# Macaron FFN, attention and RG-LRU block on one core: where the output projection's weight splits stand, and which attention unit a recurrent piece follows

## The chip, the cores and the metric

The kernel runs on one core of a Trainium2 chip. The metric is device time in microseconds (us), and lower is better. Before the change the median of three runs is 2323.7 us (2322.83 to 2324.29). Five engines with separate instruction streams share the work: TensorE (PE in the profile; its weight loads are PEld), VectorE (DVE), ScalarE (ACT), GpSimd (POOL) and SyncE (SP), whose queue issues most of the DMAs here.

## The reference, cut to what matters

The input is 1024 tokens of 1024 float32 features. One layer is computed:

```
x = LN1(ALPHA*x + 0.5 * FFN1(x))
z = x @ w_in
fox = forgetting_attention(q, k, v, fg)          # 8 heads of 64, causal, with a decay per token
lru = gelu(z_lg) * rg_lru(conv(z_lx))            # recurrent half, 512 channels
x = LN2(ALPHA*x + concat([fox, lru]) @ w_out)    # the output projection
x = LN3(ALPHA*x + 0.5 * FFN2(x))
```

The output projection is a sum of two parts: rows 0 to 511 of `w_out` multiply the attention's result, rows 512 to 1023 the recurrent result.

## The kernel before

**Three products for one.** Every large product is made of three TensorE matmuls in a 32-bit format with shorter mantissa (`mm3`, lines 156 to 158). An operand is first split into a high and a low part: ScalarE casts the high part (line 148 or 283), VectorE subtracts it from the source to get the low part (line 149 or 284). The matmuls are high x high, high x low and low x high.

**Stages.** FFN1's up and gate products, FFN1's down product, the input projection with the recurrent unit (`mixer_in`), the attention with the output projection (`attention`), then FFN2 in the same two stages. The change is in `attention`.

**Units.** The attention of one head is cut into 8 units of 128 query rows. Unit (h, i) is head h with query rows i*128 to i*128+127, and sees (i+1)*128 keys. Units are numbered n = 0 to 63 in the order of the loop. Heads 0 to 5 come one after the other, each from i = 7 (1024 keys) down to i = 0 (128 keys), so n = 24 to 31 is head 3, 32 to 39 head 4, 40 to 47 head 5. The units of heads 6 and 7 are mixed: n = 48 to 51 are (6,7) to (6,4), then (7,7), (7,6), (6,3), (6,2), (7,5), (7,4) and so on.

**What a unit does.** TensorE makes the scores (lines 999 and 1000) into one of two score tiles `s`. VectorE adds the decay and takes the minimum in one pass (line 1005, `low` below; the profile calls it CUSTOM_DVE_ANT_0). ScalarE takes the exponential (line 1006). In heads 0 to 3 VectorE takes a reciprocal (line 1008) and GpSimd multiplies with it (line 1009). Three units later (two from head 4 on) TensorE transposes the result (line 1020), ScalarE casts the high part out of PSUM (line 1024) and VectorE makes the low part (line 1025). After each second unit of a head come the products with v (line 1041), whose two halves ScalarE and VectorE put together (lines 1044 and 1045). From head 5 on two more transposes bring in the reciprocals (line 1050, used on line 1051). At the end of a head pair the result is split into the `mix` tiles (lines 1053 and 1054), and for heads 0 to 5 it is stored to DRAM (line 1057).

**Pieces in between.** The recurrent rows of the output projection do not depend on the attention. They are cut into 16 pieces (8 row blocks x 2 column halves), each 12 matmuls into one PSUM bank and one VectorE add into the residual row (`down_tile`, line 222). The loop issues a piece after chosen units, so that TensorE has work while the unit's chain runs on other engines. Before, the rule is `n < 2 or n % 8 in (2, 3, 4)`, which gives n = 0 to 4, 10 to 12, 18 to 20, 26 to 28, 34 and 35.

**The attention rows.** The weights of the other half, `w_out` rows 0 to 511, are split in four steps (`out_w`, which calls `split_ws`): each is one ScalarE cast and one VectorE subtraction of 128 x 1024. The generator is advanced at n = 45, 47, 49 and 51. The `mix` results of heads 0 to 5 are loaded back from DRAM at the units in `MIXES` (line 1110); these tiles and the weight tiles reuse the memory of the recurrent tiles, so they have to wait for the last recurrent piece that reads them. After head 7's unit (7,6) the first output tiles follow: 12 matmuls per tile (lines 156 to 158 again, now with `w` of the attention rows and `mix`), two tiles per row block, then the layer norm.

**What sets the order.** The Tile layer places the instructions of each engine by its own estimate of when their operands are ready; the order of the code is a preference. `issue_after` and `issue_behind` (the latter adds a dependence without a semaphore) force an order on one engine. Each engine then runs its stream in order, and waits on semaphores. So the place of a split in the loop does not say where it stands in the ScalarE and VectorE streams, and the trace of before shows the four splits well ahead of n = 45.

Of the kernel before, what the change touches and what calls it, by code (L numbers as in the profile page):

```python
# [12 lines left out]
AF = mybir.ActivationFunctionType  # L13
ALU = mybir.AluOpType
# [34 lines left out]
def f32(ap):  # L49
    return ap.bitcast(F32)  # L50


class Block:
# [91 lines left out]
    def split_ws(self, src, k):  # L145

        hi, lo = (self.wsp.tile([P, 4 * VW], F32R, tag="ws", name=self.nm("w"))[:, 0:D].rearrange("p (k c) -> p k c", k=k) for _ in range(2))
        self.nc.scalar.copy(hi, src)
        self.nc.vector.tensor_tensor(lo, src, f32(hi), ALU.subtract)
        return hi, lo  # L150

    def mm3(self, out, lhs, rhs, first, last, goes_on=False):
# [810 lines left out]
    def attention(self, w_out, mixp, ln, normed):  # L963

        nc, v = self.nc, self.nc.vector
# [5 lines left out]
        with self.pool("att_p", 3) as pp, self.pool("att_t", 1) as tp, self.pool("att_pt", 6) as ptp, self.pool("att_qk", 2, side="right") as qkp:  # L971

            def load(h):
                vt = qkp.tile([P, NT, P], F32R, tag="v", name=self.nm("v"))
                cum = qkp.tile([P, T], F32, tag="cum", name=self.nm("cum"))
                q, kh, kl = (qkp.tile([P, T], F32R, tag=t, name=self.nm(t)) for t in ("q", "kh", "kl"))
                mine = slice(64 * (h % 2), 64 * (h % 2) + 64)
                for j in range(2):
                    rows = slice(64 * j, 64 * j + 64)
                    nc.sync.dma_start(f32(q[rows]), self.q_d[h // 2, j, mine, :])  # L980
                    nc.sync.dma_start(f32(kh[rows]), self.k_d[h // 2, 0, mine, :])
                    nc.sync.dma_start(f32(kl[rows]), self.k_d[h // 2, 1, mine, :])
                row = self.cum_d[h:h + 1, :]
                nc.sync.dma_start(cum, bass.AP(tensor=row.tensor, offset=row.offset, ap=[[0, P], [1, T]]))
                self.last_load = nc.sync.dma_start(f32(vt), self.v_d[h].rearrange("(j p) d -> p j d", p=P))
                return q, kh, kl, vt, cum

            sums, inv = self.fgz, self.wf.rearrange("p h i -> p (h i)").rearrange("p (h i) -> p h i", h=HEADS)

            def probs(h, i):  # L990

                q, kh, kl, _, cum = heads[h]
                n = (i + 1) * P
                ts = slice(i * P, n)
                s = self.s_tile()
                for bank in range((n + H - 1) // H):
                    c1 = min(max(n - bank * H, 256), H)
                    cols = slice(bank * H, bank * H + c1)
                    mm(s[:, bank, 0:c1], q[:, ts], kh[:, cols], start=True, stop=False)
                    scores = mm(s[:, bank, 0:c1], q[:, ts], kl[:, cols], start=False, stop=True)  # L1000
                sf = s.rearrange("p b c -> p (b c)")
                p = pp.tile([P, T], F32, tag="p", name=self.nm("p"))
                nc.gpsimd.affine_select(cum[:, ts], cum[:, ts], pattern=[[-1, P]], compare_op=ALU.is_ge, fill=1e30, base=0, channel_multiplier=1)
                m = self.small.tile([P, 4], F32, tag="m", name=self.nm("m"))
                v.tensor_tensor_reduce(p[:, 0:n], sf[:, 0:n], cum[:, 0:n], 1.0, 3e38, ALU.add, ALU.min, m[:, 1:2])
                nc.scalar.activation(p[:, 0:n], p[:, 0:n], AF.Exp, bias=m[:, 1:2], scale=-1.0, accum_out=sums[:, h, i:i + 1])
                if h < LAST:
                    v.reciprocal(m[:, 3:4], sums[:, h, i:i + 1])
                    nc.gpsimd.tensor_scalar(p[:, 0:n], p[:, 0:n], m[:, 3:4], 1.0, op0=ALU.mult, op1=ALU.mult)
                return p, scores  # L1010

            def to_pT(h, i, p):
                if i % 2:
                    pts[h, i // 2] = [tuple(ptp.tile([P, 4, 256], F32R, tag="pt", name=self.nm("pt")) for _ in range(2))
                                      for _ in range((i + 4) // 4)]
                for g in range((i + 4) // 4):
                    js = range(4 * g, min(4 * g + 4, i + 1))
                    pa = self.a_tile()
                    for j in js:
                        nc.tensor.transpose(pa[:, (j % 4) * P:(j % 4 + 1) * P], p[:, j * P:(j + 1) * P], self.ident)  # L1020
                    w = len(js)
                    pav = pa.rearrange("p (j t) -> p j t", j=4)[:, 0:w, :]
                    hi, lo = (x[:, 0:w, (i % 2) * P:(i % 2 + 1) * P] for x in pts[h, i // 2][g])
                    nc.scalar.copy(hi, pav)
                    v.tensor_tensor(lo, pav, f32(hi), ALU.subtract)
                if h > LAST and h % 2 and i % 2 == 0:
                    r = inv[:, h - 1:h + 1, i:i + 2]
                    v.reciprocal(r, sums[:, h - 1:h + 1, i:i + 2])
                    nc.gpsimd.tensor_copy(self.gate_raw.rearrange("p u (b d) -> p u b d", b=2),
                                          r.rearrange("p b u -> p u b").unsqueeze(3).to_broadcast([P, 2, 2, 64]))  # L1030
# [28 lines left out]
            heads, pts, ps, outs, mixes = {}, {}, {}, {}, {}  # L1059
# [2 lines left out]
            units += [(6 + h, i) for h, i in ((0, 7), (0, 6), (0, 5), (0, 4), (1, 7), (1, 6), (0, 3), (0, 2),  # L1062
                                              (1, 5), (1, 4), (0, 1), (0, 0), (1, 3), (1, 2), (1, 1), (1, 0))]
            tiles, mix, w_fox, w_steps = [], [], [], self.out_w(w_out, 0)
            MIXES = 40, 50, 52
            fill = [(i, d) for i in range(NT) for d in range(2)]
            AHEAD, LAST = 3, 4

            def due(n):

                return [u for u in (n - AHEAD, n - AHEAD + 1) if 0 <= u < len(units) and u + AHEAD - (u >= LAST * NT) == n]
# [3 lines left out]
            def out_tile():  # L1075
                i, d = tiles.pop(0)
                self.down_tile(i, list(zip(mix + [mixes[3]], w_fox)), 1.0, (d,))
                if d:
                    self.layer_norm(i)
                    normed(i)  # L1080

            for n in range(len(units) + AHEAD + 1):
                if n < len(units):
                    h, i = units[n]
                    if i == 5 and h < 6 or (h, i) == (6, 6):
                        heads[h + 1] = load(h + 1)
                    if i == NT - 1:
                        if h % 2 == 0:
                            outs[h // 2] = tp.tile([P, T], F32, tag="o", name=self.nm("o"))
                        else:  # L1090
                            mixes[h // 2] = tuple(mixp.tile([P, T], F32R, tag="h", name=self.nm("mix")) for _ in range(2))
                    ps[n], scores = probs(h, i)
                for m in due(n):
                    to_pT(*units[m], ps.pop(m))
                for m in due(n - 1):
                    h, i = units[m]
                    if i % 2 == 0:
                        values(h, i // 2)
                        if h == HEADS - 1:
                            tiles += [(i + 1, 0), (i + 1, 1), (i, 0), (i, 1)]  # L1100
                if fill and (n < 2 or n % 8 in (2, 3, 4)):
                    i, d = fill.pop(0)
                    with self.tc.issue_after(scores.ins) if n < 3 else nullcontext():
                        self.down_tile(i, lru_tiles, 1.0, (d,))
                if 45 <= n < 53 and n % 2:
                    w_fox.append(next(w_steps))
                if n in MIXES:
                    mix.append(tuple(self.hp.tile([P, T], F32R, tag="h", name=self.nm("mix")) for _ in range(2)))
                    for l in range(2):
                        nc.sync.dma_start(f32(mix[-1][l]), mix_d[len(mix) - 1][l])  # L1110
                    if len(mix) == 3:
                        self.load_gb(*ln, [self.hp.tile([P, T], F32, tag="h", name=self.nm("gb")) for _ in range(2)])
                if tiles:
                    out_tile()
# [136 lines left out]
```

## Time and profile before

| quantity | value |
|---|---|
| median of 3 runs | 2323.7 us |
| the profiled execution's own time | 2323.84 us |
| its span, first to last instruction | 2322.1 us |
| TensorE busy | 2302.8 us |
| VectorE busy | 1631.8 us |
| ScalarE busy | 1012.6 us |
| granted TensorE clock | 0.999 |

The span is 1.7 us shorter than the profiled execution's own time. Busy times are read with care on TensorE: matmuls are pipelined, so a row of the timeline starts before the one ahead of it has ended (the modelled end), and a short wait can hide under a modelled end. The distance from one start to a later start is the safer measure, and it is used below for whole stretches between the score matmuls of two units. A row of the timeline gives start, duration, engine, line, operation, tiles and count; in brackets stands idle time ahead of it with what ended it.

### The profile page before, as it was taken

To read this page: it belongs to the slowest core of one execution; us is meant where nothing else is said; L and a number is where in the kernel's file an instruction comes from. 1 tells how busy PE (TensorE), PEld (TensorE's weight loads), DVE (VectorE), ACT (ScalarE), POOL (GpSimd) and SP (SyncE) were. 2 spreads that over 40 slices of the span, in tenths; PEclk is the share of its full clock that TensorE was granted. 3 is DMA by queue.
4 is the path that set the end of the run, shared out by engine and by line. 5 is a ranking of instruction groups with operands and counts; after the bars stand their busy time and mean duration, and the time that the engine had idled before them with its cause. 6 is when DMAs were issued, how large, how long until landed. Compare 5 with 4: busy or idle time off the path is not lost.

```text
span 2322.1 us, 28275 instructions
## 1 busy us (share of the span) xinstructions
PE 2302.8 (99%) x10737; PEld 1916.8 (83%) x10737; DVE 1631.8 (70%) x2489; ACT 1012.6 (44%) x1589; POOL 202.7 (9%) x344
## 2 busy tenths in 40 slices
PE   9999999999999999999999999999999999999998
PEld 7888888888888888888898787888888888888887
DVE  8766566666567788866667899665656665577886
ACT  5443333333344335454456745434333333344342
POOL 0020000000000000111133200000000000000000
PEclk9999999999999999999999999999999999999999
DMA  4333232323375433132275812232323232564542
GB/s 145 129 94 119 87 118 87 118 87 118 125 265 200 163 127 120 65 103 96 101 203 146 245 64 94 88 118 88 122 93 124 87 118 87 193 246 169 182 144 73
DMA packets 175976, 298.93 MB, mean 129 GB/s; under 512 B 8208, under 2 KB 100688, under 8 KB 175840
## 3 DMA queue, kind: packets, MB, share of 16 engines
q1 hardware_dynamic: 152768, 218.16, 28.9%
q0 software_dynamic: 23072, 78.97, 8.6%
q8 instruction: 84, 1.38, 0.2%
q14 instruction: 52, 0.43, 0.1%
HBM read 214.22 MB, written 82.87 MB: 128 GB/s over the span
## 4 chain that ended last, share of the span: by engine, by line
PE 93%; DVE 4%; ACT 1%; DMA 1%; issue 1%; SPq 0%; DVEq 0%; ACTq 0%
PE x L156 9%; PE x L158 9%; PE x L157 9%; PE b L156 7%; PE b L157 7%; PE b L158 7%; PE s L157 6%; PE s L158 6%; PE s L156 6%; PE a L158 6%; PE a L156 6%; PE a L157 6%; PE a L1041 1%; PE a L1020 1%; PE a L898 1%
## 5 line engine op out<-in xcount | busy, mean ns | idle before, releaser
L283 ACT CAST ws<-t 128x512 fp32r<-128x512 f32 x240 | 149.1, 623 | 394.6 <-PE b L157 267.3
L283 ACT CAST ws<-raw 128x512 fp32r<-128x512 f32 x180 | 112.0, 623 | 258.2 <-PE x L157 256.8
L284 DVE TENSOR_TENSOR ws<-raw,ws 128x512 fp32r<-128x512 f32 x180 | 123.9, 688 | 141.3 <-ACT ws L283 137.9
L284 DVE TENSOR_TENSOR ws<-t,ws 128x512 fp32r<-128x512 f32 x240 | 164.5, 686 | 70.4 <-ACT ws L283 68.5
L156 PE MATMUL b<-As,ws 128*128 128x512 f32 x512 | 199.6, 390 | 0.8 <-ACT row L517 0.4
L157 PE MATMUL a<-ws,ws 128*128 128x512 f32 x512 | 199.6, 390 | 0.2
L156 PE MATMUL a<-ws,ws 128*128 128x512 f32 x512 | 199.3, 390 | 0.5 <-ACT row L526 0.5
L157 PE MATMUL b<-As,ws 128*128 128x512 f32 x512 | 199.5, 390 | 0.0
L156 PE MATMUL x<-As,ws 128*128 128x512 f32 x512 | 199.3, 389 | 0.0
L158 PE MATMUL b<-As,ws 128*128 128x512 f32 x512 | 199.3, 389 | 0.0
L158 PE MATMUL a<-ws,ws 128*128 128x512 f32 x512 | 199.2, 389 | 0.0
L158 PE MATMUL x<-As,ws 128*128 128x512 f32 x512 | 199.2, 389 | 0.0
L157 PE MATMUL x<-As,ws 128*128 128x512 f32 x512 | 199.2, 389 | 0.0
L156 PE MATMUL x<-A,ws 128*128 128x512 f32 x496 | 193.3, 390 | 0.1
L158 PE MATMUL x<-A,ws 128*128 128x512 f32 x496 | 193.1, 389 | 0.0
L157 PE MATMUL x<-A,ws 128*128 128x512 f32 x496 | 193.0, 389 | 0.0
L621 ACT CAST ws<-raw 128x1024 fp32r<-128x1024 f32 x112 | 117.4, 1050 | 159.3 <-PE a L157 88.1
L624 DVE TENSOR_TENSOR ws<-raw,ws 128x1024 fp32r<-128x1024 f32 x112 | 136.6, 1221 | 53.0 <-ACT ws L621 52.5
L556 POOL DMA_DIRECT2D h_d<-row x96 | 68.8, 719 | 1147.2 <-DVE row L550 1108.1
L156 PE MATMUL s<-ws,ws 128*128 128x512 f32 x384 | 149.5, 389 | 0.0
L158 PE MATMUL s<-ws,ws 128*128 128x512 f32 x384 | 149.4, 389 | 0.0
L157 PE MATMUL s<-ws,ws 128*128 128x512 f32 x384 | 149.4, 389 | 0.0
(255 smaller groups left out, 5210.5 us busy)
## 6 DMA issues: line engine op xcount, KB each, us to landing
raw<-h_d SPq DMA_DIRECT2D x56, 1024.0 KB, 5.4
h_d<-row POOLq DMA_DIRECT2D x96, 512.0 KB, 3.4
wd<-in_ffn_w_down_dram SPq DMA_DIRECT2D x32, 1024.0 KB, 7.6
raw<-in_ffn_w_gate_dram SPq DMA_DIRECT2D x30, 1024.0 KB, 5.1
raw<-in_ffn_w_up_dram SPq DMA_DIRECT2D x30, 1024.0 KB, 5.2
h_d<-row POOLq DMA_DIRECT2D x32, 256.0 KB, 2.4
raw<-in_w_in_dram SPq DMA_DIRECT2D x16, 512.0 KB, 4.7
row<-in_x_dram SPq DMA_DIRECT2D x12, 512.0 KB, 8.4
```

Of the source, the lines that this page charges most:

```text
L156: mm(out, ah, bh, start=first, stop=False, skip_group_check=goes_on)
L157: mm(out, ah, bl, start=False, stop=False, skip_group_check=goes_on)
L158: mm(out, al, bh, start=False, stop=last, skip_group_check=goes_on)
L283: nc.scalar.copy(hi, src)
L284: v.tensor_tensor(lo, src, f32(hi), ALU.subtract)
L556: nc.gpsimd.dma_start(d[:, 2 * n:2 * n + 2], t.rearrange("p (r t) -> p r t", r=2))
L621: cast = nc.scalar.copy(hi, src)
L624: self.mark = v.tensor_tensor(lo, src, f32(hi), ALU.subtract)
L898: nc.tensor.matmul(pa[:, 0:width], xh, wh[:, 0:width], start=k == 0, stop=False)
L1020: nc.tensor.transpose(pa[:, (j % 4) * P:(j % 4 + 1) * P], p[:, j * P:(j + 1) * P], self.ident)
L1041: mm(pv[:, ps], vt[:, j, :], pts[h, qt][j // 4][l][:, j % 4, ps], start=j == 0 and l == 0, stop=j == last and l == 1)
```

## The change

Four edits, all in the attention stage:

- The pieces of the recurrent rows follow a list of units now. It is the old one without n = 27 (head 3) and with n = 42 (head 5).
- The generator of the weight splits is advanced at n = 47, 49, 51 and 53 (before 45 to 51). Its cast is tied behind the exponential of that unit on ScalarE, and its subtraction behind that unit's `low` on VectorE.
- The load of the first mixed pair moves from n = 40 to n = 43 (the last recurrent piece that reads the tiles it reuses is now at n = 42).
- `split_ws` and `probs` hand out their instructions so that they can be tied.

```diff
     def split_ws(self, src, k):
...
-        self.nc.scalar.copy(hi, src)
-        self.nc.vector.tensor_tensor(lo, src, f32(hi), ALU.subtract)
+        self.split_ops = (self.nc.scalar.copy(hi, src),
+                          self.nc.vector.tensor_tensor(lo, src, f32(hi), ALU.subtract))
         return hi, lo
...
-                v.tensor_tensor_reduce(p[:, 0:n], sf[:, 0:n], cum[:, 0:n], 1.0, 3e38, ALU.add, ALU.min, m[:, 1:2])
-                nc.scalar.activation(p[:, 0:n], p[:, 0:n], AF.Exp, bias=m[:, 1:2], scale=-1.0, accum_out=sums[:, h, i:i + 1])
+                low = v.tensor_tensor_reduce(p[:, 0:n], sf[:, 0:n], cum[:, 0:n], 1.0, 3e38, ALU.add, ALU.min, m[:, 1:2])
+                exp = nc.scalar.activation(p[:, 0:n], p[:, 0:n], AF.Exp, bias=m[:, 1:2], scale=-1.0, accum_out=sums[:, h, i:i + 1])
...
-            MIXES = 40, 50, 52
+            MIXES = 43, 50, 52
             fill = [(i, d) for i in range(NT) for d in range(2)]
+            FILLS = 0, 1, 2, 3, 4, 10, 11, 12, 18, 19, 20, 26, 28, 34, 35, 42
...
-                if fill and (n < 2 or n % 8 in (2, 3, 4)):
+                if n in FILLS:
                     i, d = fill.pop(0)
...
-                if 45 <= n < 53 and n % 2:
+                if 47 <= n < 55 and n % 2:
                     w_fox.append(next(w_steps))
+                    for part, op in zip(self.split_ops, ops):
+                        self.issue_behind(part, op)
```

Three places show what becomes of the order. The first is TensorE's stream in head 5 before the change, from the scores of unit 42 (`s_10838`) to those of unit 43 (`s_10875`); `a_10854` and `a_10861` are the transposes of unit 40, `a_10868` the products with v that close head 4.

```order
L999 MATMUL s_10838<-kh_10549,q_10548 128x512
L1000 MATMUL s_10838<-kl_10550,q_10548 128x512
L999 MATMUL s_10838<-kh_10549,q_10548 128x256
L1000 MATMUL s_10838<-kl_10550,q_10548 128x256
L1020 MATMUL a_10854<-ident,p_10780 128x128 x4
L1020 MATMUL a_10861<-ident,p_10780 128x128 x4
L999 MATMUL s_10875<-kh_10549,q_10548 128x512
L1000 MATMUL s_10875<-kl_10550,q_10548 128x512
L999 MATMUL s_10875<-kh_10549,q_10548 128x256
L1000 MATMUL s_10875<-kl_10550,q_10548 128x256
L1041 MATMUL a_10868<-pt_10787,v_10248 128x256
```

The same place after the change, from the transposes of unit 40 (`a_10836`, `a_10843`) to the scores of unit 43 (`s_10871`); `a_10857` is the recurrent piece.

```order
L1020 MATMUL a_10836<-ident,p_10766 128x128 x4
L1020 MATMUL a_10843<-ident,p_10766 128x128 x4
L1041 MATMUL a_10850<-pt_10773,v_10248 128x256
...
L156 MATMUL a_10857<-w_9256,mix_7242 128x512
L157 MATMUL a_10857<-w_9257,mix_7242 128x512
L158 MATMUL a_10857<-w_9256,mix_7243 128x512
...
L158 MATMUL a_10857<-w_9270,mix_8641 128x512
L999 MATMUL s_10871<-kh_10535,q_10534 128x512
L1000 MATMUL s_10871<-kl_10536,q_10534 128x512
```

The 12 matmuls of the piece stand between the scores of units 42 and 43 now, behind the products with v.

The second place is VectorE's stream before the change from the `low` of unit 48 (line 1005, 128x1024) to that of unit 50 (128x768).

```order
L1005 ISA p_11050,m_11054<-s_11045,cum_10826 128x1024
L1005 ISA m_11054 128x1
L1051 TENSOR_TENSOR o_10495<-o_10495,a_11016 128x256
L1025 TENSOR_TENSOR pt_10993<-a_11032,pt_10992 128x3x128
L1025 TENSOR_TENSOR pt_11058<-a_11059,pt_11057 128x2x128
L1005 ISA p_11099,m_11103<-s_11094,cum_10826 128x896
L1005 ISA m_11103 128x1
L1045 TENSOR_TENSOR o_10495<-o_10495,a_11064 64x256
L1025 TENSOR_TENSOR pt_11058<-a_11106,pt_11057 128x128
L1051 TENSOR_TENSOR o_10495<-o_10495,a_11075 128x256
L1005 ISA p_11123,m_11127<-s_11118,cum_10826 128x768
```

The same units after the change, with the first two of the four splits (line 149, `w` from `raw`).

```order
L1005 ISA p_11046,m_11050<-s_11041,cum_10808 128x1024
L1005 ISA m_11050 128x1
L149 TENSOR_TENSOR w_11037<-raw_11034,w_11036 128x1024
L1025 TENSOR_TENSOR pt_11054<-a_11055,pt_11053 128x2x128
L1005 ISA p_11095,m_11099<-s_11090,cum_10808 128x896
...
L1051 TENSOR_TENSOR o_10481<-o_10481,a_11071 128x256
L1005 ISA p_11117,m_11121<-s_11112,cum_10808 128x768
L1005 ISA m_11121 128x1
L1025 TENSOR_TENSOR pt_11125<-a_11128,pt_11124 128x4x128
L149 TENSOR_TENSOR w_11109<-raw_11034,w_11108 128x1024
L1005 ISA p_11166,m_11170<-s_11161,cum_10808 128x640
```

Splits that stood in heads 4 and 5 before stand behind the `low` of units 48 and 50 now; the third and fourth follow behind units 51 and 54.

The third place is VectorE's stream ahead of the first output tile before the change; `pt_11288` and `pt_11290` are the low parts that the products with v of the first tile's rows read, the `low` of 128x768 is that of unit 56.

```order
L1025 TENSOR_TENSOR pt_11290<-a_11298,pt_11289 128x4x128
L1045 TENSOR_TENSOR o_11044<-o_11044,a_11305 64x256
L1005 ISA p_11350,m_11354<-s_11345,cum_11082 128x768
L1005 ISA m_11354 128x1
L1025 TENSOR_TENSOR pt_11288<-a_11330,pt_11287 128x4x128
L1025 TENSOR_TENSOR pt_11290<-a_11337,pt_11289 128x3x128
L1025 TENSOR_TENSOR pt_11358<-a_11359,pt_11357 128x4x128
L1005 ISA p_11410,m_11414<-s_11405,cum_11082 128x640
```

The same place after the change, with the fourth split in the first row.

```order
L149 TENSOR_TENSOR w_11274<-raw_11186,w_11273 128x1024
L1025 TENSOR_TENSOR pt_11290<-a_11298,pt_11289 128x4x128
L1045 TENSOR_TENSOR o_11040<-o_11040,a_11305 64x256
L1005 ISA p_11323,m_11327<-s_11320,cum_10808 128x384
L1005 ISA m_11327 128x1
L1025 TENSOR_TENSOR pt_11288<-a_11330,pt_11287 128x4x128
L1025 TENSOR_TENSOR pt_11290<-a_11337,pt_11289 128x3x128
L1028 RECIPROCAL wfr<-fgz 128x2x2
L1005 ISA p_11350,m_11354<-s_11345,cum_11078 128x768
L1005 ISA m_11354 128x1
```

The `low` of unit 56 stands behind the two low parts now that the products with v wait for, and not ahead of them.

In SP's stream the loads of head 6's q, k, v and decay come ahead of the loads of the first two mixed pairs now; before they stood behind them.

More of the change, by code (lines that the diff above doesn't have):

```diff
@@ L1009, in probs @@
                     nc.gpsimd.tensor_scalar(p[:, 0:n], p[:, 0:n], m[:, 3:4], 1.0, op0=ALU.mult, op1=ALU.mult)
-                return p, scores
+                return p, scores, (exp, low)
             def to_pT(h, i, p):
@@ L1091, in attention @@
                             mixes[h // 2] = tuple(mixp.tile([P, T], F32R, tag="h", name=self.nm("mix")) for _ in range(2))
-                    ps[n], scores = probs(h, i)
+                    ps[n], scores, ops = probs(h, i)
                 for m in due(n):
```

## The prediction

> **What bounds the kernel now.** I read the page first: how full each engine is, and the chain that ended last.
>
> ```profile
> PE 2302.8 (99%) x10737; PEld 1916.8 (83%) x10737; DVE 1631.8 (70%) x2489; ACT 1012.6 (44%) x1589; POOL 202.7 (9%) x344
> ...
> PE 93%; DVE 4%; ACT 1%; DMA 1%; issue 1%; SPq 0%; DVEq 0%; ACTq 0%
> ```
>
> TensorE bounds the kernel, and no matmul is added or taken away. So the change can only alter how long TensorE waits inside the attention. Next come the timeline's rows at which I cut the attention: the first score matmul of units 26, 34, 42 and 50 and the first output tile, and in between one recurrent piece.
>
> ```profile
> 1249.22 0.50 PE L999 MATMUL s<-kh,q 128*128 128x512 f32 x1 [0.18 <-DVE m L1005]
> ...
> 1255.57 0.45 PE L156 MATMUL a<-w,mix 128*128 128x512 f32 x1
> ...
> 1258.37 0.39 PE L999 MATMUL s<-kh,q 128*128 128x512 f32 x1
> ...
> 1271.31 0.50 PE L999 MATMUL s<-kh,q 128*128 128x512 f32 x1 [0.31 <-DVE m L1005]
> ...
> 1292.45 0.50 PE L999 MATMUL s<-kh,q 128*128 128x512 f32 x1
> ...
> 1308.30 0.50 PE L999 MATMUL s<-kh,q 128*128 128x512 f32 x1 [0.31 <-DVE m L1005]
> ...
> 1328.63 0.48 PE L156 MATMUL a<-w,mix 128*128 128x512 f32 x1
> ```
>
> A piece holds TensorE from 1255.57 to 1258.37, that is 2.80 us. Eight units take 22.09 us in head 3 (units 26 to 33) with three pieces, 21.14 with two (34 to 41) and 15.85 with none (42 to 49). Without its pieces head 3 takes 22.09 - 3 x 2.80 = 13.69 us; I call this the bare pace. Against it units 34 to 41 lose 21.14 - 5.60 - 13.69 = 1.85 us, and units 42 to 49 lose 15.85 - 13.69 = 2.16. The windows view of the same stretches says which engine is full there (columns: length, then busy us of PE, PEld, DVE, ACT, POOL).
>
> ```profile
> core 0: us, PE busy (x) PEld busy (x) DVE busy (x) ACT busy (x) POOL busy (x), PEclk, DMA share, GB/s
> ...
> 1249.22:1271.31 22.09, 21.78 (x136) 19.31 (x136) 16.54 (x45) 14.11 (x36) 8.24 (x16) 1.00 0.46 119
> 1271.31:1292.45 21.14, 20.38 (x131) 17.85 (x131) 19.62 (x42) 17.30 (x38) 3.57 (x10) 1.00 0.72 221
> 1292.45:1308.30 15.85, 14.79 (x97) 11.82 (x96) 14.38 (x38) 13.10 (x34) 5.09 (x12) 1.00 0.98 246
> 1308.30:1328.63 20.33, 19.45 (x138) 16.41 (x138) 18.49 (x42) 17.45 (x40) 6.80 (x17) 1.00 0.92 290
> ```
>
> VectorE has 5.55 us free in head 3 (22.09 - 16.54), but only 1.52, 1.47 and 1.84 us in the three stretches behind it. From unit 34 to the first output tile VectorE is the engine that sets the pace.
>
> **The splits leave heads 4 and 5.** The windows of line 149 (the subtraction, on VectorE) tell where they are:
>
> ```profile
> 1271.31:1292.45 21.14, 3.66 (x3) 1.00 0.72 221
> 1292.45:1308.30 15.85, 1.22 (x1) 1.00 0.98 246
> ```
>
> And those of line 148 (the cast, on ScalarE):
>
> ```profile
> 1271.31:1292.45 21.14, 4.21 (x4) 1.00 0.72 221
> ```
>
> Three of the four subtractions (3.66 us) and all four casts (4.21 us) stand in units 34 to 41. The timeline shows how a cast reaches TensorE, first on ScalarE, then on TensorE:
>
> ```profile
> 1288.32 1.06 ACT L148 CAST w<-raw 128x1024 fp32r<-128x1024 f32 x1
> 1289.27 0.41 ACT L1006 ACTIVATE p<-p,m 128x128 f32<-128x128 f32 x1
> ...
> 1290.19 0.76 ACT L1024 CAST pt<-a 128x384 fp32r<-128x384 f32 x2
> ```
>
> ```profile
> 1286.75 0.39 PE L1041 MATMUL a<-pt,v 128*128 128x256 f32 x1 [0.39 <-ACT pt L1024]
> ...
> 1290.72 0.39 PE L1041 MATMUL a<-pt,v 128*128 128x256 f32 x1 [0.37 <-ACT pt L1024]
> ```
>
> The products with v waited 0.39 and 0.37 us for the cast of the transposed rows, which stood in ScalarE's queue behind a split's cast. Taken away, VectorE has 19.62 - 3.66 = 16.0 us of work in a stretch that TensorE cannot do in less than 13.69 + 5.60 = 19.3. TensorE then bounds it. At most the 1.85 us come back; late in the stretch no piece covers the chain, so I take 1.6 (bounds 0.8, twice the two waits' 0.38, and 1.85).
>
> **The piece leaves head 3.** This stretch gets shorter by 2.80 us, if TensorE stays the bound: 19.3 us, with VectorE at 16.54 less one row add, so still some 3 us free. I take 2.7 (bounds 2.5 and 2.8).
>
> **The piece enters head 5.** It stands between the scores of units 42 and 43. TensorE's floor for units 42 to 49 becomes 13.69 + 2.80 = 16.5 us, 0.65 above today's 15.85: it fills the 2.16 us that VectorE made TensorE wait. VectorE loses a split there (1.22) and gets the piece's add, so its 14.38 us do not grow; but its stream runs dry while TensorE does the piece, since the add stands ahead of the next `low`. I take +0.8 (bounds +0.5 and +1.8, the upper one if VectorE idles some 1.2 us and TensorE gets it all).
>
> **The splits enter units 48 to 55.** This is the costly step. Behind a split queue the low parts of the transposed rows (line 1025), for which the products with v wait, and the next `low`, for which the scores two units on wait, since there are two score tiles. One VectorE split took from 1293.81 to the next start at 1294.95:
>
> ```profile
> 1293.81 1.22 DVE L149 TENSOR_TENSOR w<-raw,w 128x1024 fp32r<-128x1024 f32 x1
> 1294.95 0.41 DVE L1045 TENSOR_TENSOR o<-o,a 64x256 f32<-64x256 f32 x1
> ...
> 1325.02 0.96 DVE L1005 CUSTOM_DVE_ANT_0 p<-s,cum 128x768 f32<-128x768 f32 x1
> 1325.90 1.75 DVE L1025 TENSOR_TENSOR pt<-a,pt 128x512 fp32r<-128x512 f32 x3
> ```
>
> That is 1.14 us, four times 4.56, in a stretch where VectorE has 1.84 us free. In full this costs 4.56. Filling all its gaps it would cost 2.7. One reordering helps: the `low` of unit 56 (0.88 us from 1325.02 to 1325.90) no longer stands ahead of the low parts that the last products with v ahead of the output tile read. So the bounds are 1.8 and 4.6. The gaps have these releasers (VectorE's waits, then TensorE's, from unit 50 into the first output tile):
>
> ```profile
> DVE o L1045 <- ACT o L1044: 1.3, 3, 0.8
> DVE wfr L1028 <- ACT p L1006: 1.1, 1, 1.1
> ```
>
> ```profile
> PE s L999 <- DVE m L1005: 0.7, 2, 0.4
> PE a L158 <- DVE mix L1054: 0.4, 1, 0.4
> ```
>
> The 1.3 us are VectorE waiting for the end of products with v. A VectorE that is later has that work ready when it comes, so these gaps shrink; the 1.1 us behind the exponential lie next to the output tile and are partly covered too. I take 2.5, nearer the lower end.
>
> **Edits at nothing.** The four casts on ScalarE (4.21 us) go into a stretch with 20.33 - 17.45 = 2.9 us free and stand behind the exponentials; their cover is VectorE, which is fuller, and without it they'd cost up to the two waits' 0.76 us again. The loads of the mixed pair (n = 43) and of head 6 change places in SP's queue; both are needed only at unit 48 and later. FFN2's first weights now wait in SP's queue for the splits to free their buffer, and the last mixed pair is queued behind them; they are used behind the 16 output tiles, 16 x 2.80 = 45 us later. Without that cover a load would stand bare:
>
> ```profile
> raw<-in_ffn_w_gate_dram SPq DMA_DIRECT2D x30, 1024.0 KB, 5.1
> ```
>
> That is 5.1 us from issue to landing.
>
> **The sum.** -2.7 - 1.6 + 0.8 + 2.5 = -1.0 us. The profiled execution took 2323.84 us (its span 2322.1 and 1.7 around it), 0.14 above the median of the runs. So the forecast is 2323.7 - 1.0 = 2322.7 us. A measurement of this kernel can tell about 0.2%, that is 4.6 us, from no change, so I forecast no change that can be told.
>
> [...] At the first output tile a VectorE subtraction met a GpSimd multiplication:
>
> ```profile
> 1331.01 1.04 POOL L185 TENSOR_SCALAR gb<-gb 128x1024 f32<-128x1024 f32 x1 [4.66 <-DMA gb<-in_ln_g_dram]
> 1331.25 1.07 DVE L1054 TENSOR_TENSOR mix<-o,mix 128x256 fp32r<-128x256 f32 x1 [0.47 <-ACT mix L1053]
> ```
>
> The view of the tile gives the group's shortest, median and longest (ns):
>
> ```profile
> L1054 DVE TENSOR_TENSOR mix<-o,mix x12: 402/420/1070, 1223.2 to 1370.7; 128x256 fp32r<-128x256 f32 x12
> ```
>
> It took 1.07 us where the median of its group is 0.42, and ended just behind GpSimd's. The split's subtraction reads two operands from the same memory as this one, and GpSimd is busy for 6.80 us in units 50 to 55, against 3.57 in units 34 to 41, where three of the splits were. A split that meets such an operation would cost up to 1.07 - 0.42 = 0.65 us more. [...]
>
> **The rivals.**
>
> - *The splits fit into the gaps.* Heads 4 and 5 run at the bare pace, and units 50 to 55 pay only 0.9 us, because each split falls where VectorE waits for ScalarE. -2.8 - 1.85 + 0.65 + 0.9 = -3.1: 2320.6 us. For it: the ties put each split behind the operation on which the scores hang. Against: 1.84 us of gaps for 4.56 us of work. Chance 0.2.
> - *VectorE is the bound, and the splits cost in full* (slower). Place: units 48 to 55; price 4.56. It decides as soon as they cost more than 2.7 + 1.6 - 0.8 = 3.5 us. -2.7 - 1.6 + 0.8 + 4.6 = +1.1: 2324.8 us. For it: 18.49 of 20.33 us busy. Against: the gaps that end on ScalarE's copy. Chance 0.17.
> - *The splits meet GpSimd* (slower). Each of the four is held 0.65 us: -1.0 + 2.6 = +1.6, 2325.3 us. Against: it needs a meeting each time, and GpSimd's 6.80 us there are 17 operations, 0.4 us each. Chance 0.13.
> - That the change doesn't do what it says is ruled out by the order, where all four splits stand behind unit 48's `low`.
>
> **How the numbers follow.** The forecast keeps 0.5. The range reaches from the first rival with its lower bounds, 2319.8, to the third with 0.7 us on top, 2326.0. Over 0.2% faster (below 2319.1) needs the first rival and the output tile's waits gone besides: 0.07. Over 0.2% slower (above 2328.3) needs the second and third together: 0.03. The rest, 0.90, is within 0.2%.
>
> **What would show it right or wrong.** Right: units 26 to 33 take 19.4 us, 34 to 41 19.5, 42 to 49 16.6, and unit 50 to the first output tile 22.8; line 149 has no row before unit 48; no wait of the products with v for line 1024 in head 4. Wrong: head 4 stays above 20.5 (the splits weren't its brake), units 42 to 49 go above 17.5 (the piece starves VectorE), or the last stretch stays below 21.5 or goes above 25; a row of line 149 near 1.9 us would be the meeting with GpSimd.

## The result, and the profile after

The kernel after the change takes 2327.5 us (median of 20 runs, 2325.6 to 2329.4), the kernel before 2323.6 in the same session: a ratio of 1.0018 (95% interval 1.0012 to 1.0024), 3.9 us slower. That is less than the 0.2% which the prediction took for the least that can be told, but the interval stays above 1. The profiled execution took 2327.54 us, its span 2325.8.

The page first: busy time by engine, and the shares of the chain that ended last.

```profile
PE 2304.2 (99%) x10737; PEld 1917.8 (82%) x10737; DVE 1632.3 (70%) x2489; ACT 1012.4 (44%) x1589; POOL 202.2 (9%) x344
...
PE 93%; DVE 4%; DMA 1%; ACT 1%; issue 1%; POOL 0%; SPq 0%; DVEq 0%; ACTq 0%; POOLq 0%
```

The work is the same. The one new thing is small: GpSimd (POOL) is now on the chain, with a share that rounds to 0%. The timeline's rows at the cuts of the prediction (first score of units 26, 34, 42 and 50, first output tile):

```profile
1248.75 0.50 PE L999 MATMUL s<-kh,q 128*128 128x512 f32 x1 [0.18 <-DVE m L1005]
...
1268.88 0.50 PE L999 MATMUL s<-kh,q 128*128 128x512 f32 x1 [0.31 <-DVE m L1005]
...
1288.51 0.50 PE L999 MATMUL s<-kh,q 128*128 128x512 f32 x1
...
1307.07 0.48 PE L999 MATMUL s<-kh,q 128*128 128x512 f32 x1
...
1331.31 0.51 PE L156 MATMUL a<-w,mix 128*128 128x512 f32 x1
```

The first cut lies 0.47 us earlier than before, ahead of anything that was changed. The cut of unit 26 lies between 1248.5 and 1250.6 us in the profiles of most kernels below, so lengths are compared and not times of day. The windows of the four stretches:

```profile
1248.75:1268.88 20.13, 19.54 (x124) 17.07 (x124) 15.84 (x44) 13.92 (x36) 8.24 (x16) 1.00 0.56 137
1268.88:1288.51 19.63, 19.61 (x125) 16.98 (x125) 15.91 (x38) 13.49 (x34) 3.57 (x10) 1.00 0.62 176
1288.51:1307.07 18.56, 18.41 (x125) 16.33 (x126) 16.09 (x41) 14.99 (x36) 5.72 (x15) 1.00 0.88 250
1307.07:1331.31 24.24, 19.48 (x128) 15.60 (x126) 20.94 (x42) 19.74 (x42) 7.50 (x16) 1.00 0.92 295
```

Together they hold 502 matmuls, as before (136 + 131 + 97 + 138). But the cuts lie elsewhere in TensorE's stream now: beside the 12 of the piece, units 42 to 49 hold 16 more than before, six taken from head 4 and ten from the last stretch. So single stretches are only roughly comparable; their sums are exact: 79.41 us before, 82.56 after, +3.15.

Most of it is one wait. TensorE's waits from unit 50 on, and then GpSimd's timeline there:

```profile
PE a L1050 <- POOL gate_raw L1029: 2.1, 1, 2.1
```

```profile
1326.36 0.29 POOL L1003 TENSOR_SCALAR_AFFINE_SELECT cum<-cum 128x128 f32<-128x128 f32 x1 [3.51 <-DVE m L1005]
1329.67 1.04 POOL L185 TENSOR_SCALAR gb<-gb 128x1024 f32<-128x1024 f32 x1 [3.02 <-DMA gb<-in_ln_g_dram]
1330.67 0.39 POOL L1029 COPY gate_raw<-wfr 128x256 f32<-128x256 f32 x1
1331.03 0.28 POOL L1003 TENSOR_SCALAR_AFFINE_SELECT cum<-cum 128x128 f32<-128x128 f32 x1
```

GpSimd stood for 3.02 us at line 185, the multiplication of the layer norm's gain (`gb`) by -1, because the gain's load had not landed. Behind it stood the copy of the gates (line 1029), which the first output tile needs, and the affine select of unit 57. They started at 1330.67 and 1331.03, each as soon as the one ahead of it was through, so both waited for a load that they don't need. Before the change the copy and the select of unit 57 ran far ahead of it:

```profile
1323.99 0.40 POOL L1029 COPY gate_raw<-wfr 128x256 f32<-128x256 f32 x1
1326.06 0.29 POOL L1003 TENSOR_SCALAR_AFFINE_SELECT cum<-cum 128x128 f32<-128x128 f32 x1 [1.67 <-DVE m L1005]
```

Neither the diff's lines nor its words name GpSimd. The scheduler placed the multiplication two places earlier as a side effect, ahead of the copy and of the select of unit 57. GpSimd's stream there, before and after (in each list the first select is that of unit 57):

```
L1029 COPY gate_raw<-wfr 128x256
L1003 AFFINE_SELECT cum<-cum 128x128
L185 TENSOR_SCALAR gb<-gb 128x1024
L1003 AFFINE_SELECT cum<-cum 128x128
```

```
L185 TENSOR_SCALAR gb<-gb 128x1024
L1029 COPY gate_raw<-wfr 128x256
L1003 AFFINE_SELECT cum<-cum 128x128 x2
```

Behind the wait of 2.06 us TensorE's clock fell from 1.00 to 0.50. The windows around the first output tile, in which the last three columns are the granted clock, the DMA share and GB/s, and then TensorE's rows at the wait and behind it:

```profile
1326.00:1331.11 5.11, 3.03 (x22) 2.60 (x20) 2.90 (x8) 2.74 (x7) 1.73 (x4) 1.00 0.97 337
...
1332.00:1333.00 1.00, 1.00 (x4) 0.76 (x3) 0.86 (x4) 0.73 (x1) 0.29 (x1) 0.50 0.34 122
1333.00:1334.00 1.00, 1.00 (x4) 0.81 (x3) 0.71 (x3) 0.59 (x3) 0.40 (x1) 0.50 0.02 6
...
1335.10:1340.00 4.90, 4.90 (x30) 4.20 (x29) 2.81 (x7) 0.72 (x2) 0.00 (x0) 1.00 0.00 0
```

```profile
1331.11 0.44 PE L1050 MATMUL a<-ident,gate_raw 128*128 128x128 f32 x2 [2.06 <-POOL gate_raw L1029]
...
1331.62 0.63 PE L157 MATMUL a<-w,mix 128*128 128x512 f32 x1
1332.04 0.63 PE L158 MATMUL a<-w,mix 128*128 128x512 f32 x1
```

The matmuls of the output tile start 0.42 to 0.43 us apart where a piece before the change has 0.23: eight matmuls at 0.2 us more, 1.6 us. From the first output tile to FFN2's first matmul it is 59.15 us before (1328.63 to 1387.78) and 60.10 after (1331.31 to 1391.41), 0.95 more, since some waits of before are gone there. 3.15 + 0.95 - 0.47 = 3.63 us, and the span grew by 3.7.

### The profile page after: what moved, and what is told of

It reads as the page before. It is cut to its first block, busy times and chain, and to the rows that moved or that the text cites. A ratio compares the mean times of both kernels' runs of the same rounds, so it can differ in the third digit from the quotient of the medians.

```text
span 2325.8 us, 28275 instructions
## 1 busy us (share of the span) xinstructions
PE 2304.2 (99%) x10737; PEld 1917.8 (82%) x10737; DVE 1632.3 (70%) x2489; ACT 1012.4 (44%) x1589; POOL 202.2 (9%) x344
## 4 chain that ended last, share of the span: by engine, by line
PE 93%; DVE 4%; DMA 1%; ACT 1%; issue 1%; POOL 0%; SPq 0%; DVEq 0%; ACTq 0%; POOLq 0%
PE x L158 10%; PE x L156 10%; PE x L157 9%; PE b L156 7%; PE b L157 7%; PE b L158 7%; PE s L158 6%; PE s L157 6%; PE s L156 6%; PE a L158 6%; PE a L156 6%; PE a L157 6%; PE a L1041 1%; PE a L1020 1%; PE a L898 1%
## 5 line engine op out<-in xcount | busy, mean ns | idle before, releaser
L621 ACT CAST ws<-raw 128x1024 fp32r<-128x1024 f32 x112 | 117.4, 1050 | 159.3 <-PE a L157 88.2
```

The source lines that it names most:

```text
L621: cast = nc.scalar.copy(hi, src)
```

## The experiments

Two theories. *GpSimd's order*: the loss is the multiplication ahead of the copy and the select, and the clock behind it. *The splits*: they make VectorE and ScalarE late in units 48 to 57, and another wait would take that one's place. Kernels with added lines have other line numbers: where `gb` is line 192, the scores are 1005, the `low` 1011, the copy 1035.

**The copy alone put ahead.** The changed kernel, the multiplication tied behind the gate copy:

```
+                if n == 56:
+                    self.flip_gb()                  # the multiplication of line 185
+                    self.issue_behind(self.flip, self.gate_copy)
```

> The changed kernel with one instruction moved: GpSimd's multiplication of the layer norm's gain (gb, line 185) is tied behind the copy of the reciprocals (gate_raw) that feeds the two transposes ahead of the first output tile; the streams of TensorE, VectorE and ScalarE stay word for word the same. Theory A (the loss is this order on GpSimd: the copy stood behind a multiplication that waited for its DMA; TensorE stood still for 2.1 us, its clock fell to half for some 3.7 us, which is another 1.6 us): the wait of line 1050 for gate_raw is gone, the clock is 1.00 throughout, and the time is 2.1 + 1.6 = 3.7 us lower than the changed kernel's, 2323.8 us, not to be told from before. Theory B (the four splits on VectorE and ScalarE in units 48 to 55 are the loss, the wait for GpSimd only shows where it ends): the wait moves to another releaser and the time stays at 2327 to 2328 us.

Measured: 2327.8 us, ratio 1.0017 (1.0008 to 1.0026). No gain. The copy ran at 1328.27, but the select of unit 57 was still behind:

```profile
1331.14 1.05 POOL L192 TENSOR_SCALAR gb<-gb 128x1024 f32<-128x1024 f32 x1 [2.47 <-DMA gb<-in_ln_g_dram]
1332.15 0.29 POOL L1009 TENSOR_SCALAR_AFFINE_SELECT cum<-cum 128x128 f32<-128x128 f32 x1
```

```profile
PE a L156 <- ACT mix L1059: 2.7, 1, 2.7
```

The `low` of unit 57 waited for that select, and in VectorE's and ScalarE's queues the mix's cast stood behind it. As far as this run goes either theory could be right: a wait did take the other's place.

**The order of GpSimd alone.** The kernel before, its copy tied behind the multiplication:

```
+                    if (h, i) == (HEADS - 1, 6):
+                        self.issue_behind(copy, self.flip)
```

> The kernel before with one instruction moved: the same copy of the reciprocals is tied behind GpSimd's multiplication of the gain, as the changed kernel has it; nothing else is changed, and the streams of TensorE, VectorE and ScalarE are those of before. Theory A: the copy waits for the gain's DMA (landed at about 1331 us in the trace of before, the products with v end at 1328.5): a wait of 2 to 3 us at line 1050, the clock at half behind it, and 3.5 to 5 us more than before, 2327 to 2328.5 us. Theory B: without the moved splits nothing is lost beyond a short wait; at most 1 us more than before, 2323.5 to 2324.5 us.

Measured: 2328.0 us, 1.0018 (1.0009 to 1.0027), as the first theory had it. GpSimd and TensorE (line 1052 is line 1050 of the kernel before):

```profile
1330.47 1.04 POOL L185 TENSOR_SCALAR gb<-gb 128x1024 f32<-128x1024 f32 x1 [4.35 <-DMA gb<-in_ln_g_dram]
1331.47 0.39 POOL L1029 COPY gate_raw<-wfr 128x256 f32<-128x256 f32 x1
```

```profile
1331.91 0.45 PE L1052 MATMUL a<-ident,gate_raw 128*128 128x128 f32 x2 [3.47 <-POOL gate_raw L1029]
```

No split and no piece moved, and the loss is as large as that of the whole change. So this order is enough for it.

**Each half of the change.** The piece and the first mixed pair moved, the splits as before; then the splits tied, the rest as before:

```
-            MIXES = 40, 50, 52
+            MIXES = 43, 50, 52          # and the last piece at unit 42, none at 27
```

> Only the recurrent piece is moved from unit 27 to 42 and the first mixed pair from 40 to 43; the splits stand as before. In its GpSimd stream the multiplication of the gain stands behind the copy of the reciprocals. Theory A: no stall at line 1050; the piece fills waits of TensorE in head 5, so the time is 0.5 to 2 us below before: 2321.5 to 2323 us. Theory B says the same of this one (the splits are not moved), so it only gives the piece's own part.

```
-                if 45 <= n < 53 and n % 2:
+                if 47 <= n < 55 and n % 2:   # and the two ties behind exp and low
```

> Only the splits are tied to units 47 to 53; the piece stays at unit 27, the first mixed pair at 40. In its GpSimd stream the multiplication of the gain stands ahead of the copy, as in the changed kernel. Theory A: the stall at line 1050 and the half clock are there again; 3.5 to 5.5 us above before, 2327 to 2329 us, with the clock below 1.00 around the first output tile. Theory B: also slower, by the splits' own cost of 2.5 to 4.6 us, 2326 to 2328 us, but with no long wait at line 1050.

Measured: the piece alone 2325.1 us, 1.0004 (0.9995 to 1.0013), above the 2321.5 to 2323 expected; the splits alone 2328.6, 1.0019 (1.001 to 1.0028). In the first, units 42 to 49 took 21.70 us:

```profile
1290.26:1311.96 21.70, 19.23 (x126) 16.27 (x126) 19.83 (x44) 17.89 (x40) 6.78 (x13) 1.00 0.94 259
```

All four splits are there now, behind the `low` of units 42 to 47, although their place in the program didn't move. In every kernel here they come behind the last piece; that they wait for the buffers of its weights is likely, but was not tried by itself. In the second kernel the multiplication stood ahead of the copy again, with a wait of 1.0 us. The time is in the range that the first theory gave, but the clock stayed at 1.00, and so short a wait can't be the whole loss of 5 us; the price of the splits is measured below.

**GpSimd's order put right.** The changed kernel, the multiplication tied behind copy and select, so that GpSimd's order there is that of before and the other engines' streams are those of after:

```
+                if n == 57:
+                    self.flip_gb()
+                    self.issue_behind(self.flip, self.select)   # the affine select of unit 57
```

> The changed kernel with GpSimd's gain multiplication tied behind the gate copy and the affine select of unit 57, so that GpSimd's order there is that of the kernel before; the streams of TensorE, VectorE and ScalarE are those of the changed kernel. GpSimd theory (both the copy and the select were held by a multiplication that waits for a DMA): the wait of TensorE for the gate copy (2.1 us) and the slow clock behind it (8 matmuls, 0.2 us each) both go, no wait over 0.5 us takes their place at the first output tiles, 2327.5 - 2.1 - 1.6 = 2323.8 us (bounds 2323.3 and 2324.8). Rival (the splits of the projection's weights make VectorE late, and the next wait in line takes the place again): 2326.5 to 2327.8.

Measured: 2324.6 us, 1.0002 (0.9993 to 1.0011). GpSimd, then the windows of the last stretch and behind it:

```profile
1328.43 0.40 POOL L1035 COPY gate_raw<-wfr 128x256 f32<-128x256 f32 x1 [0.92 <-DVE wfr L1034]
1329.22 0.29 POOL L1009 TENSOR_SCALAR_AFFINE_SELECT cum<-cum 128x128 f32<-128x128 f32 x1 [0.39 <-DVE m L1011]
1331.05 1.05 POOL L192 TENSOR_SCALAR gb<-gb 128x1024 f32<-128x1024 f32 x1 [1.54 <-DMA gb<-in_ln_g_dram]
```

```profile
1307.92:1329.90 21.98, 19.28 (x128) 15.55 (x126) 21.09 (x43) 19.00 (x40) 6.57 (x15) 1.00 0.83 277
1329.90:1335.00 5.10, 5.10 (x26) 3.82 (x25) 3.87 (x9) 2.54 (x7) 1.84 (x3) 1.00 0.69 249
```

GpSimd still waits for the load (1.54 us), but with nothing behind it that anyone needs. The last stretch has 21.98 us in place of 24.24, the clock stays at 1.00, and no other wait comes in. This is the first theory, 2.9 us of the 3.9.

**The clock.** The changed kernel, with work that nobody reads in the place of the wait:

```
+                        if (h, qt) == (HEADS - 1, 3):
+                            for _ in range(22):
+                                nc.tensor.transpose(pr[:, 256:384], self.ident, self.ident)
```

> The changed kernel with 22 transposes of the identity put on TensorE ahead of the two gate transposes of the first output tile, 2.1 us of work that nobody reads, in the place of the 2.1 us in which TensorE stood. Clock theory (the granted clock halves because TensorE stood still): the output tile starts when it did, or up to 0.3 us later, the granted clock stays 1.00 behind it, and the eight matmuls at 0.427 us go back to 0.2275: 2327.5 - 1.6 = 2325.9 us (bounds 2325.5 and 2326.5). Rival (the low clock there has another cause, such as the load on the chip's power at that moment): the low clock is there again and the time is 2327.5 to 2328.

```profile
1328.90:1331.11 2.21, 2.21 (x23) 2.21 (x22) 0.55 (x1) 1.39 (x3) 1.45 (x3) 1.00 1.05 389
...
1333.00:1334.00 1.00, 1.00 (x6) 0.75 (x4) 0.60 (x2) 0.30 (x3) 0.40 (x1) 1.00 0.01 2
```

The granted clock stays at 1.00 where it was 0.50, so at this place it is TensorE's standing still, for 2.06 us, that costs the clock. The time missed its bounds: 2327.5 us, 1.0016 (1.0007 to 1.0024), no gain that can be told. The profiled execution (2326.9) is 1.1 us shorter from unit 26 on. Whether other executions of the changed kernel have the slow clock as well stays open.

**The price of the splits and the piece.** The kernel before with the splits tied and the multiplication put right:

> The kernel before with only the four splits tied to units 47 to 53 (no piece moved, first mixed pair as before), and the gain multiplication of GpSimd put behind the select of unit 57. With the multiplication in the way these splits gave 2328.6 us. If the splits cost by themselves what they hold up on VectorE, only the 1.05 us wait for the gate copy goes: 2327.3 us (bounds 2326.6 and 2327.8). Rival (the splits are hidden in VectorE's gaps and all of the loss was GpSimd's order): 2323.7 us.

Measured: 2326.8 us, 1.0011 (1.0002 to 1.002); the forecast of the first kind holds, so without the piece in head 5 the splits cost some 3 us by themselves. From unit 34 to the first output tile this kernel takes 60.52 us (1271.18 to 1331.70); the changed kernel with the multiplication right takes 60.23 (1269.67 to 1329.90), though TensorE does a piece of 2.8 us more there. So the piece in head 5 costs nothing once the splits stand behind it. Then the changed kernel with the multiplication right, first without the subtractions on VectorE, then with no split at all:

```
+        if not low:
...
+            self.split_ops = (self.nc.scalar.copy(hi, src),)
+            return hi, hi
```

> The changed kernel with GpSimd's order put right (2324.6 us), and the four splits without their subtraction on VectorE: the low part of the projection's attention weights is left out (the high part stands in its place), the casts on ScalarE and all matmuls stay. If the subtractions cost what they hold up on VectorE (2.8 us of lost TensorE time in units 50 to 57 against the kernel before, four subtractions of 1.14 us), these go: 2324.6 - 2.8 = 2321.8 us (bounds 2320.1, all four in full, and 2322.8). Rival (it is the casts on ScalarE, or the later loads, that hold TensorE up there): 2324 to 2325 us.

```
-                    w_fox.append(next(w_steps))      # and its ties
+                    w_fox.append(lru_tiles[len(w_fox)][1])
```

> The changed kernel with GpSimd's order put right and no split of the attention rows' weights at all: their loads, casts and subtractions are left out, and the output tiles take the recurrent rows' parts in their place, with as many matmuls. Without the four subtractions alone the time was 2323.3 us, and from unit 50 to the first output tile 20.9 us. If the four casts on ScalarE (1.05 us each, ahead of the next casts of the transposed rows) are the rest of what this stretch pays (1.6 us above the kernel before): 2323.3 - 1.6 = 2321.7 us (bounds 2321.0 and 2322.6). Rival (the casts lie in ScalarE's gaps, and the rest comes from the order of the scores, transposes and products, or from the piece in head 5): 2322.9 to 2323.7 us, and the stretch stays within 0.4 us of 20.9.

Measured: 2323.3 us, 1.0000 (0.9991 to 1.0009), and 2322.2 us, 0.9992 (0.9983 to 1.0001), the second within its bounds. The last stretch of the one, and all four of the other:

```profile
1307.77:1328.63 20.86, 19.29 (x130) 15.50 (x128) 17.50 (x39) 19.30 (x42) 5.54 (x14) 1.00 0.91 296
```

```profile
1249.20:1269.32 20.12, 19.54 (x124) 17.07 (x124) 15.83 (x44) 13.91 (x36) 8.31 (x16) 1.00 0.54 131
1269.32:1288.98 19.66, 19.65 (x124) 17.00 (x125) 15.92 (x38) 13.50 (x34) 3.59 (x10) 1.00 0.64 176
1288.98:1307.54 18.56, 18.40 (x125) 16.33 (x126) 15.77 (x41) 14.15 (x35) 5.52 (x15) 1.00 0.88 252
1307.54:1327.11 19.57, 18.30 (x129) 15.71 (x128) 17.59 (x39) 16.82 (x39) 5.49 (x14) 1.00 0.85 269
```

So the subtractions cost 21.98 - 20.86 = 1.1 us, not the 2.8 that I had expected here, and casts and loads with them another 20.86 - 19.57 = 1.3. The medians differ by about as much, but their intervals overlap; the stretch of 21.98 us has the same length in the profile with the copy alone put ahead (1307.76 to 1329.74), whose TensorE, VectorE and ScalarE do the same in the same order. In both kernels the scheduler also exchanges some scores and transposes in TensorE's stream, so neither figure is the subtractions' or the casts' alone.

**Other places for the splits.** The pieces of head 4 moved to heads 1 and 2, the splits tied to units 31 to 37:

```
+            FILLS = 0, 1, 2, 3, 4, 10, 11, 12, 13, 18, 19, 20, 21, 26, 27, 28
+                if 31 <= n < 39 and n % 2:
```

> The kernel before with the recurrent pieces of head 4 moved to heads 1 and 2 (last piece at unit 28), the four splits tied to units 31 to 37 and the gain multiplication behind the select of unit 57. The splits can't start before the last recurrent piece has given its weights' buffers back. If the splits cost where VectorE has no room, and head 3 has room (5.5 us free), one split less stands in head 5 and heads 3 and 4 run near the bare pace: 2322.3 us (bounds 2321.0 and 2323.7). Rival (head 4 needs its two pieces as cover for VectorE's chain; without them it loses the up to 2.2 us that head 5 lost): 2324.5 to 2325.9 us.

Measured: 2329.3 us, 1.0023 (1.0014 to 1.0032), slower than the rival had it: head 4 without its pieces and with splits took 20.09 us, with a longest wait of 1.6.

The subtractions on GpSimd, in the changed kernel with the multiplication right and in the kernel before:

```
+                          (eng or self.nc.vector).tensor_tensor(lo, src, f32(hi), ALU.subtract)
```

> The changed kernel with GpSimd's order put right (2324.6 us), and the four subtractions of the splits on GpSimd in place of VectorE. VectorE theory: VectorE gets 4 x 1.14 us back, and GpSimd, with 7.5 of 24 us busy there, takes four operations of some 2 us each (a 128x256 subtraction there takes 0.8 us): 2322.2 us (bounds 2321.0 and 2323.5). Rival (GpSimd's selects, its copy of the gates and its low part of the mix now queue behind these subtractions, as they did behind the gain multiplication): 2325.5 to 2328 us, with waits on GpSimd's operations of over 1 us.

> The kernel before with the four subtractions of the same splits on GpSimd in place of VectorE, at the place where they were (units 35 to 42), GpSimd's order of the gain multiplication unchanged. If VectorE holds TensorE up in heads 4 and 5 and the subtractions are part of it (2.5 and 4.0 us of lost TensorE time there): 2322.0 us (bounds 2320.5 and 2323.0). Rival (GpSimd's selects queue behind the subtractions and the next score waits for them): 2324.0 to 2326.5 us.

Measured: 2325.1 us, 1.0006 (0.9997 to 1.0015), and 2325.4 us, 1.0007 (0.9998 to 1.0017): the first just under the rival's range, the second in it. On GpSimd one takes 2.4 us, twice VectorE's 1.22, and the copy of the gates stands behind it (rows of the first):

```profile
1325.61 2.38 POOL L149 TENSOR_TENSOR w<-raw,w 128x1024 fp32r<-128x1024 f32 x1 [1.02 <-ACT w L148]
1327.93 0.40 POOL L1035 COPY gate_raw<-wfr 128x256 f32<-128x256 f32 x1
```

None of the kernels that do the whole computation beat the kernel before.

## Why the prediction was wrong

It said 2322.7 us, with a range up to 2326.0; it was 2327.5. By its own steps, in the profiled executions ("order put right" is the experiment of that name above):

| step | forecast | measured | from |
|---|---|---|---|
| piece leaves head 3 | -2.7 | -1.96 | 22.09 to 20.13 |
| splits leave heads 4, 5; piece enters head 5 | -1.6 + 0.8 = -0.8 | +0.47 | 57.32 to 57.79, units 34 to the first output tile without any split |
| splits enter units 48 to 55 | +2.5 | +2.44 | 57.79 to 60.23, with GpSimd's order put right |
| everything else ("at nothing") | 0 | +2.20 | 60.23 to 62.43, the multiplication ahead |
| behind the first output tile: waits of before that are gone | 0 | -0.38 | 59.15 to 58.77, with GpSimd's order put right |
| the slow clock there | 0 | +1.33 | 58.77 to 60.10, the multiplication ahead (58.88 with the wait covered) |
| earlier start | 0 | -0.47 | not of the change |
| sum | -1.0 | +3.63 | |

**The step that failed is "edits at nothing".** It went through ScalarE's casts, SP's queue and FFN2's weights, and never looked at GpSimd's stream, though there the order of the changed program shows the multiplication ahead of the copy. The trace of before had the price at hand: the prediction itself quotes the row in which that multiplication waits 4.66 us for its load, and cost it only as a neighbour of VectorE. The multiplication was moved with its wait: 3.02 us of it stood ahead of the copy now. That step, with the slow clock behind it, was 2.20 + 1.33 = 3.53 of the 4.63 us by which the sum was off. None of the three rivals had this cause.

**Head 3** gave 0.7 us less. Where the piece left, TensorE stands now. From the first of seven transposes (1255.62) to the next piece (1257.21) TensorE needs 1.59 us for them and one score matmul, which before took 0.68 + 0.17 = 0.85. The row of the wait there, and VectorE's row of the `low` ahead of it:

```profile
1255.35 0.82 DVE L1005 CUSTOM_DVE_ANT_0 p<-s,cum 128x640 f32<-128x640 f32 x1 [1.33 <-PE a L1041]
```

```profile
1256.93 0.52 PE L1020 MATMUL a<-ident,p 128*128 128x128 f32 x3 [0.26 <-DVE pt L1025]
```

The prediction argued from VectorE's 5.5 us of free time. Part of that is time like these 1.33 us, in which VectorE stood and waited for TensorE; the low part (line 1025) for which the transposes waited was queued behind this `low`.

**Heads 4 and 5** gave 1.3 us less. The prediction read "VectorE is the engine that sets the pace" from its busy time. What such a reading is worth shows in the last stretch: VectorE was busy there for 21.09 of 21.98 us with the subtractions and for 17.50 of 20.86 without them, so 3.6 us less work brought 1.1. In heads 4 and 5 no run takes work from VectorE alone: with the subtractions on GpSimd units 34 to 41 took 22.65 us, against 21.14 before. The piece's entry isn't what fell short: with the splits late it made units 34 to the first output tile 0.3 us shorter (60.52 to 60.23), where +0.8 was forecast. What the splits' leaving brought there by itself no run shows, and so the cause of this 1.3 us stays open.

**The splits** cost what was forecast, 2.4 for 2.5, but only 1.1 of it on VectorE; the casts, which the prediction costed at nothing by themselves, lie in the other 1.3. So the size was right partly by luck: of its working only the smaller half holds.

The rivals. *The splits fit into the gaps* and *VectorE is the bound* (0.9 and 4.6 us for the splits) both fell. *The splits meet GpSimd* fell in its price: the view of the tile's line gives shortest, median and longest of line 149 as

```profile
L149 DVE TENSOR_TENSOR w<-raw,w x24: 1171/1224/1344, 917.4 to 1323.6; 128x1024 fp32r<-128x1024 f32 x24
```

with no row near 1.9 us. The meetings did take place, but what took longer beside a split was for the most part GpSimd's operation:

```profile
1306.32 1.34 DVE L149 TENSOR_TENSOR w<-raw,w 128x1024 fp32r<-128x1024 f32 x1
```

```profile
1306.53 1.28 POOL L1003 TENSOR_SCALAR_AFFINE_SELECT cum<-cum 128x128 f32<-128x128 f32 x1
```

A select that takes 0.29 us elsewhere took 1.28 and ended 0.15 us behind the split that had started before it, which itself took 1.34 where the median is 1.22. Beside the third split, at 1.22, GpSimd's low part of the mix took 1.08 us where the others take 0.74. Of TensorE's waits in these stretches none ends on GpSimd but the one for the gates.

Of the signs, units 26 to 33 (19.4 forecast, 20.13) and 34 to 41 (19.5, 19.63) stayed below the bounds named as wrong. Units 42 to 49, at 18.56 where 16.6 was forecast, went above the 17.5; but by an estimate about 1.8 us of that are the 16 matmuls that come from the neighbours (products with v start some 0.12 us apart), so the sign can't be read. The last stretch, at 24.24, stayed under the 25 named as wrong, and 2.2 of it were the wait.

## What to carry to other kernels

When a change makes a scheduler reorder the program, compare every engine's stream, the idle ones first: an engine that is 9% busy can still hold the kernel up, if one of its instructions waits for a load and what others need is queued behind it (here TensorE stood for 2.06 us). Tie such an instruction behind the last one that somebody waits for. And a busy engine is a bound only if taking work from it shortens the path (here 3.6 us less work for VectorE brought 1.1): test that before you pay for moving the work.

## What the runs showed of the hardware

The slow clock doesn't follow from the length of a wait alone. The clock fell to 0.50 behind a wait of 2.06 us (the changed kernel) and behind one of 3.47 (the copy tied behind the multiplication), but stayed at 1.00 behind 2.72 (the copy alone put ahead). In the kernel with early splits it fell behind two short waits, of 0.53 and 0.87 us. The slow stretch lasted 3.41 us in the changed kernel and with early splits; with the copy tied behind the multiplication it was about 3.4, by an estimate from the mean clock there (0.55 over 1332.00 to 1334.00, 0.80 over 1334.00 to 1338.00). First the 3.41 us ahead of the fall and the slow stretch in the changed kernel, then the same in the kernel with early splits:

```profile
1328.20:1331.61 3.41, 1.35 (x11) 1.18 (x10) 0.97 (x4) 1.39 (x3) 1.64 (x3) 1.00 0.97 351
1331.61:1335.02 3.41, 3.41 (x9) 2.63 (x8) 2.20 (x6) 1.32 (x3) 0.69 (x2) 0.50 0.16 55
```

```profile
1276.79:1280.20 3.41, 2.01 (x12) 1.48 (x11) 3.35 (x7) 2.29 (x5) 0.41 (x1) 1.00 1.04 214
1280.20:1283.61 3.41, 3.41 (x17) 3.22 (x16) 2.40 (x7) 2.86 (x6) 0.59 (x2) 0.50 0.68 191
```

With the copy alone put ahead the clock is 1.00 in both of two stretches of that length, one from ahead of the longer wait into it, the next on from there:

```profile
1330.06:1333.47 3.41, 2.00 (x9) 1.31 (x7) 0.97 (x3) 0.49 (x3) 1.40 (x3) 1.00 0.88 312
1333.47:1336.88 3.41, 2.10 (x10) 1.57 (x11) 2.39 (x6) 1.73 (x4) 0.60 (x2) 1.00 0.04 15
```

How much TensorE works in a stretch of that length doesn't settle it either. Ahead of the two falls it was busy for 1.35 and 2.01 of 3.41 us; with the copy alone put ahead, 3.41 us that hold the whole wait have at most 3.41 - 2.72 = 0.69 us of work, and the clock stayed at 1.00. What else it takes for the clock to fall these runs don't tell.
